# Two experts' weight loads per layer placed behind the overflow branch and the first gathered tokens

## The chip, the cores and the metric

The kernel runs on one NeuronCore of a Trainium2 chip. The metric is the device time of one execution in microseconds, as the median of several runs. Matrix products run on TensorE (PE in the profile; PEld is its weight load), elementwise work on VectorE (DVE), ScalarE (ACT) and GpSimd (POOL). SyncE (SP) issues nearly all DMA transfers; POOL issues the indirect ones.

## The reference, cut to what matters

The reference is a transformer block followed by a second model of two layers. Each of these layers ends with a mixture of experts, and only that part is touched:

```python
MOE_GROUPS, MOE_EXPERTS_PER_GROUP, MOE_TOPK, D_EXPERT, D_MODEL = 4, 4, 2, 256, 1024
# a router picks a group of four experts for each token, and the best two in it
# for each token t and each of its two experts e, with weight c:
#     y[t] += c * ((silu(h[t] @ gate[e]) * (h[t] @ up[e])) @ down[e])
```

There are 16 experts; layer 0 has 768 tokens, layer 1 has 512. Everything is float32.

## The kernel before, in words

The program is one Python class that emits instructions for all engines into a tile framework. The framework inserts the semaphores from the tiles that an instruction reads and writes, and it orders the instructions of an engine by when it expects them to be ready, within what their tiles allow. So a DMA issue may stand earlier in SP's queue than where the Python code calls it, if nothing that it needs forbids it.

Each layer's expert stage has three parts.

The first, `moe_open`, `moe_chunk` and `moe_in`, runs beside and after the attention's output projection. `moe_in` finishes the router's logits; `route` turns them into a list of tokens for each slot: a prefix sum by a matmul with a triangular constant (L2410; in layer 0 the constant `tr` is loaded at L2373 and cast at L2375), a chain of small VectorE instructions, and the list `tok` (L2473). Meanwhile the normalized tokens are transposed, evicted into one of three row buffers `hgs` (L2354) and written to DRAM as `hrows` (L2355). The scaled tokens that are transposed lie in the buffers of the expert `ME[i]`, which is 2 in layer 0 and 3 in layer 1 (`mxa`).

The second, `moe`, works in blocks of 128 slots, one block for each of the 16 experts. `gather(b)` (L2589) fetches a block's rows of `hrows` by an indirect DMA on POOL into `hgs[b % 3]`. A block transposes them (L2609), splits them and the weights into a rounded part and a remainder (L106, L2580, L2581), multiplies with three matmuls for each product (L110 to L112), and scatters the result to `ybuf` (L2640). `blocks` interleaves the steps of neighbouring blocks: a block's weights are loaded up to three blocks ahead, its rows are gathered two ahead.

Before the 16 regular blocks there is a branch (L2655) on the number of overflow blocks, for experts with more than 128 tokens. With these inputs it is not taken: 32 gathers run, 16 in each layer. The gathers of blocks 0 and 1 are issued ahead of it. Its body would load experts into the buffers of expert `ov`, reload that expert afterwards and gather blocks 0 and 1 again. So what reads or writes the row buffers or `ov`'s weights after the branch can't be placed ahead of it; other work can.

The third sums up the two rows of each token from `ybuf`.

Weights: `load_expert(i, b)` issues ten loads on SP, eight for gate and up (four tiles `wgu`, two loads each, L2557) and two for down (`wd`, L2559). There are four sets of buffers (`ew`, expert `b` in set `b % 4`). The first four experts of a layer are loaded in different places:

- Layer 0: expert 0 in `moe_open`, expert 1 within the output projection, expert 3 in `moe_in`, and expert 2 (whose buffers hold the scaled tokens) in `moe` after the branch.
- Layer 1: expert 0 in the attention, expert 1 in `moe_open`, expert 2 within the output projection (after its first quarter), and expert 3 (whose buffers hold the scaled tokens) in `moe` after the branch.

Experts 4 to 15 follow as buffers come free. In the queue of SP, the eight gate and up loads of the expert that the code loads after the branch stand ahead of it, since they don't depend on it.

Of the kernel before, what the change touches and what calls it, by code (L numbers as in the profile page):

```python
# [37 lines left out]
ME = (2, 3)  # L38
# [6 lines left out]
NE, LD, NL = 4, 3, 4  # L45
# [5 lines left out]
class Model:  # L51
# [2000 lines left out]
    def layer1(self, mod):  # L2052
        nc, tc, I, c2 = self.nc, self.tc, self.I, self.c2
        X = self.X
        W = I["od_w_in_2"][0]
        self.l1w.close()
        snk = self.bcast_load(I["swa_sink_2"][0], 16, "snk1", c2)
        nsnk = self.t(c2, [128, 16], "nsnk1")
        nc.vector.tensor_scalar(nsnk, snk, -1.0, None, op0=ALU.mult)
        self.dflt = "st"  # L2060
        ep = self.l1p[1]
        bp = self.l1x.enter_context(tc.tile_pool(name="l1b", bufs=1, side="right"))
        band = self.t(bp, [128, 1664], "bandm")
        self.bandm = [band[:, 0:512], band[:, 512:1152], band[:, 1152:1664]]
        for case, m in enumerate(self.bandm):
            nc.sync.dma_start(m, I["c_band"][:, case, :m.shape[1]])
        oF = self.out_tiles(1, 2, 4)

        def q_unit(j):
            cst = self.t(ep, [128, 256], "cq", bufs=1)  # L2070

            def mm():
                raw = self.l1_load(W[:, 256 * j:256 * j + 256])
                self.l1_const(j, cst)
                while self.apr < 2 * j - 2:
                    yield
                self.newQ2(j)
                yield
                ps = self.bank("a2")
                out = [ps[:, t * 256:(t + 1) * 256] for t in range(4)]  # L2080
                for k0 in range(0, 8, 2):
                    hi, lo = (self.t(self.wp, [128, 512], t, F32R, bufs=3).rearrange("p (k n) -> p k n", n=256)
                              for t in ("whi", "wlo"))
                    self.l1_split(raw, 0, hi, lo, k0)
                    for k in range(k0, k0 + 2):
                        Hk, Lk = (T[k // 2][:, k % 2] for T in self.l1T)
                        for t in range(4):
                            sl = slice(t * 128, (t + 1) * 128)
                            for i, (a, b) in enumerate(((Hk, hi), (Hk, lo), (Lk, hi))):
                                nc.tensor.matmul(out[t], a[:, sl], b[:, k - k0], start=k == 0 and t % 2 == 0 and i == 0,  # L2090
                                                 stop=k == 7 and t % 2 == 1 and i == 2, skip_group_check=True)
                    yield
                return out

            def tile_(ps, t):
                raw = self.t(ep, [128, 256], "rawq", bufs=4)
                nc.vector.scalar_tensor_tensor(raw, ps[t], self.l1rs[:, t:t + 1], cst, op0=ALU.mult, op1=ALU.add)
                yield from self.l1_heads(raw, 4)
                yield
                yield from self.l1_queries(raw, t, self.Q2[j])  # L2100
            return ("q", j), mm, self.staged(4, tile_, 4)
        done = {("q", 0)}
        self.apr = 0
        filler = self.stream([lambda j=j: q_unit(j) for j in range(1, 4)], done, SL)
        with self.psum(st=3, s2=1, a2=1, pv=1), tc.tile_pool(name="l1a", bufs=1) as at:
            self.mark("attn1")
            self.band_attn(at, oF, snk, nsnk, filler, done)
        self.l1x.close()
        with self.psum(acc=5, lg=1, st=2):
            with tc.tile_pool(name="l1x", bufs=1) as xp:  # L2110
                self.pad(xp, 64)
                oT = (self.t(xp, [128, 8, 512], "oThi", F32R), self.t(xp, [128, 8, 512], "oTlo", F32R))
                wo = I["od_w_out_2"][0]
                first = self.primed(self.proj_feat_g(oT, [wo[:, 0:256]], 1024))
                for m in range(8):
                    self.split(oT[0][:, m, :], oT[1][:, m, :], oF(m, 0, 512))
                self.mq = xp
                self.moe_open(1, X, 4, [self.AB["f", 1, 0]])
                for nq in range(4):
                    pf = self.run_g(first) if nq == 0 else self.proj_feat(oT, [wo[:, nq * 256:(nq + 1) * 256]], 1024)  # L2120
                    for f in range(2):
                        d = nq * 2 + f
                        nc.vector.scalar_tensor_tensor(X[:, d, :512], pf[f], mod[:, 16 + d, 0:1], X[:, d, :512],
                                                       op0=ALU.mult, op1=ALU.add)
                        self.moe_chunk(d)
                    if nq == 0:
                        self.load_expert(1, 2)
            self.mark("moein1")
            self.moe_pool(1)
            self.moe_in(1)  # L2130
        self.mark("moe1")
        self.moe(1, mod, X, 4, None, None, None)
        self.xes.close()
# [159 lines left out]
    def moe_in(self, i):  # L2293

        nc, nt, lg = self.nc, self.mnt, self.lg
# [25 lines left out]
                nc.vector.tensor_reduce(L[:, n0:n0 + m], src.rearrange("p n g e -> p n e g"), axis=AX.X, op=ALU.add)  # L2321
        nc.vector.tensor_tensor(L, L, r[:, :, None].to_broadcast([128, nt, 20]), op=ALU.mult)
        nc.vector.tensor_tensor(L, L, self.lc, op=ALU.add)
        for j in range(NL):
            if j not in self.ewt and j != ME[i]:
                self.load_expert(i, j)
        self.hrows = self.dr.tile([nt * 128, 1024], F32, name=f"hrows{i}")

        rt, rth = self.t(mp, [128, nt], "rt"), self.t(mp, [128, nt, 3], "rth", F32R)
# [214 lines left out]
            return v[:, u, :] if nm is None else v[:, u:u + nm, :]  # L2544
        return at

    def load_expert(self, i, b, ev=None, into=None):

        nc, I, ep = self.nc, self.I, self.ew[b % NE]
        s1, s2 = (slice(b * n, (b + 1) * n) if ev is None else bass.ds(ev * n, n) for n in (1024, 256))  # L2550
        src = lambda nme: I[f"exp_w_{nme}_2"][i].rearrange("g e d f -> (g e d) f")
        gu, dn = into or ([self.t(ep, [128, 2, 512], f"wgu{c}") for c in range(4)],
                          [self.t(ep, [128, 1024], f"wd{k}") for k in range(2)])
        for c, w in enumerate(gu):
            for u, nme in enumerate(("gate", "up")):
                rows = src(nme)[s1, :].rearrange("(k p) n -> p k n", p=128)
                nc.sync.dma_start(w[:, :, u * 256:(u + 1) * 256], rows[:, 2 * c:2 * c + 2, :])  # L2557
        for k, w in enumerate(dn):
            nc.sync.dma_start(w, src("down")[s2, :].rearrange("(k p) n -> p k n", p=128)[:, k, :])  # L2559
        self.ewt[b] = gu, dn  # L2560

    def moe(self, i, mod, xT, nt, banks, begin, finish):
        nc, tc, I = self.nc, self.tc, self.I
# [2 lines left out]
        ybuf = self.dr.tile([2 * 768, 1024], F32, name=f"ybuf{i}")  # L2566
        hgs = self.hgs
        direct = 15 if i else None
        ov = 5 - ME[i]
        with self.ewx, tc.tile_pool(name=f"moel{i}", bufs=1) as mp, self.psum(st=3, ht=1, gu=2, yy=2):  # L2570
            self.pad(mp, 64)
            cnt = [0]
# [15 lines left out]
            def gather(b):  # L2588
                nc.gpsimd.indirect_dma_start(out=hgs[b % 3], out_offset=None, in_=self.hrows[:, :],  # L2589
                                             in_offset=bass.IndirectOffsetOnAxis(ap=self.tok[:, b:b + 1], axis=0),  # L2590
                                             bounds_check=T - 1, oob_is_err=False)
# [52 lines left out]
            def blocks(bs):  # L2644
                g = [block(b) for b in bs]
                for it in range(-3, len(g) + 2):
                    for d in (1, 0, -2, -1, 0, 2, LD):
                        if 0 <= it + d < len(g):
                            next(g[it + d], None)
# [5 lines left out]
            with tc.If(nov > 0):  # L2655
# [3 lines left out]
                self.load_expert(i, ov, into=self.ewt[ov])  # L2659
                for b in range(2):  # L2660
                    gather(b)
            self.load_expert(i, ME[i])
            blocks(range(16))
            if i:
                self.moe_end(mod, xT, ybuf, dS)
# [105 lines left out]
def host_consts():  # L2771
# [18 lines left out]
    for li, L in enumerate((64, 32, 16, 8, 4, 2, 1)):  # L2790
# [28 lines left out]
        "c_rope": np.ascontiguousarray(rope.transpose(1, 0, 2, 3)).astype(np.float32),  # L2819
        "c_band": band,  # L2820
        "c_moe": moe,
        "c_iota": np.ascontiguousarray(np.broadcast_to(a.astype(np.float32), (128, 128))),
        "c_onehot": oh,
# [28 lines left out]
```

## Time and profile before

| | |
|---|---|
| median of 3 runs | 2259.61 us (2256.55 to 2264.92) |
| profiled execution, its own time | 2261.34 us |
| its span, first to last instruction | 2259.6 us |
| TensorE busy | 94% of the span |
| granted clock, mean | 0.974 of full speed |
| expert stage of layer 0, first to last transpose of tokens | 1585.1 to about 1719 us |
| expert stage of layer 1, the same | 2077.4 to about 2211 us |

All times within the profile are counted from the span's start. A wait is named after the event that came last by the profile. `DMA share` is the mean busy share of the core's 16 DMA engines; the profile's estimate can lie a little above 1.

### The profile page before, as it was taken

What the parts mean: (1) busy time and instruction counts of PE and PEld (TensorE: products, weight loads), DVE (VectorE), ACT (ScalarE), POOL (GpSimd) and SP (SyncE); (2) the same over time, 40 slices, a digit from 0 to 9 for tenths busy, and PEclk for the clock granted to TensorE, in tenths of its full rate; (3) what the DMA queues carried; (4) which work ended last, traced back from release to release, by engine and by line L of the source; (5) the groups of instructions that cost most, each with busy time, mean ns of one, the idle gap of its engine ahead of it and who ended that gap; (6) DMA issues with size and microseconds to landing.
All of it is one profiled execution on the core that took longest, in us unless ns stands there. A gap on an engine that the chain in (4) does not pass through costs nothing. (4 is left out here: it accounts for less than half of the span.)

```text
span 2259.6 us, 36705 instructions
## 1 busy us (share of the span) xinstructions
PE 2125.8 (94%) x13410; PEld 1751.8 (78%) x13410; DVE 1401.2 (62%) x3175; ACT 1221.0 (54%) x2623; POOL 500.5 (22%) x459
## 2 busy tenths in 40 slices
PE   7999999999999999999999989896999989996997
PEld 6887775688887888888889777775787978775886
DVE  5665656555555544355631677644999777755997
ACT  4655456543334243333442676733898467654996
POOL 2222030002112212120420333100442421101442
PEclk9999999999999999999999999998999999998998
DMA  6446627553242222323112111064996411144995
GB/s 210 158 138 200 221 97 253 187 187 128 94 149 94 76 94 94 112 83 123 52 59 81 40 43 48 26 206 163 339 359 234 174 40 60 40 150 142 341 334 191
DMA packets 213120, 328.54 MB, mean 145 GB/s; under 512 B 22598, under 2 KB 150516, under 8 KB 206780
## 3 DMA queue, kind: packets, MB, share of 16 engines
q1 hardware_dynamic: 203708, 305.05, 40.3%
q0 software_dynamic: 9216, 20.99, 2.5%
q8 instruction: 109, 1.79, 0.3%
q14 instruction: 87, 0.71, 0.1%
HBM read 307.51 MB, written 31.06 MB: 150 GB/s over the span
## 5 line engine op out<-in xcount | busy, mean ns | idle before, releaser
L106 DVE TENSOR_TENSOR wlo<-wst,whi 128x512 fp32r<-128x512 f32 (+1 forms) x342 | 245.1, 722 | 418.6 <-ACT whi L105 355.8
L105 ACT CAST whi<-wst 128x512 fp32r<-128x512 f32 (+1 forms) x342 | 210.7, 619 | 486.0 <-PE acc L111 357.1
L112 PE MATMUL acc<-hThi,wlo 128*128 128x512 f32 (+2 forms) x576 | 225.3, 391 | 1.0 <-DVE wlo L106 0.9
L110 PE MATMUL acc<-hThi,whi 128*128 128x512 f32 (+2 forms) x576 | 225.0, 391 | 0.7 <-ACT ostg L633 0.7
L111 PE MATMUL acc<-hTlo,whi 128*128 128x512 f32 (+2 forms) x576 | 224.5, 390 | 0.0
L153 POOL TENSOR_TENSOR hnr<-rsq,nhalf 128x4 f32<-128x4 f32 (+3 forms) x58 | 72.2, 1245 | 266.5 <-DVE rsq L147 144.4
L218 PE MATMUL acc<-whi,hThi 128*128 128x256 f32 x416 | 122.3, 294 | 6.5 <-ACT hThi L374 6.2
L112 PEld LDWEIGHTS acc<-hThi,wlo 128*128 128x128 f32 (+2 forms) x576 | 106.8, 185 | 25.9 <-DVE wlo L106 2.5
L524 PE MATMUL pv<-PT,V 128*64 128x128 f32 x1456 | 123.1, 283 | 3.1 <-ACT PT L1469 1.7
L110 PEld LDWEIGHTS acc<-hThi,whi 128*128 128x128 f32 (+2 forms) x576 | 106.8, 185 | 24.5 <-issue 2.9
L111 PEld LDWEIGHTS acc<-hTlo,whi 128*128 128x128 f32 (+2 forms) x576 | 106.8, 185 | 20.9
L218 PE MATMUL acc<-wlo,hThi 128*128 128x256 f32 x416 | 119.9, 288 | 0.0
L218 PE MATMUL acc<-whi,hTlo 128*128 128x256 f32 x416 | 119.4, 288 | 0.0
L524 PEld LDWEIGHTS pv<-PT,V 128*64 128x64 f32 x1456 | 88.8, 138 | 28.5 <-issue 12.1
L112 PE MATMUL acc<-hMhi,wlo 128*128 128x512 f32 x256 | 99.9, 391 | 1.3 <-DVE wlo L106 1.3
L110 PE MATMUL acc<-hMhi,whi 128*128 128x512 f32 x256 | 100.2, 391 | 0.0
L111 PE MATMUL acc<-hMlo,whi 128*128 128x512 f32 x256 | 99.6, 389 | 0.0
L2581 DVE TENSOR_TENSOR elo<-wgu,ehi 128x512 fp32r<-128x512 f32 x128 | 89.2, 706 | 11.6 <-ACT ehi L2580 10.9
L218 PEld LDWEIGHTS acc<-whi,hThi 128*128 128x128 f32 x416 | 81.1, 195 | 12.1 <-ACT hThi L374 6.5
L2580 ACT CAST ehi<-wgu 128x512 fp32r<-128x512 f32 x128 | 80.8, 631 | 1.7
L2580 ACT CAST whi<-wgu 128x512 fp32r<-128x512 f32 x128 | 81.1, 634 | 0.6 <-PE gu L112 0.2
L218 PEld LDWEIGHTS acc<-wlo,hThi 128*128 128x128 f32 x416 | 81.2, 195 | 0.3 <-DVE wlo L106 0.2
(701 smaller groups left out, 6146.1 us busy)
## 6 DMA issues: line engine op xcount, KB each, us to landing
mst<-in_mod_w_dram SPq DMA_DIRECT2D x48, 1024.0 KB
wgu<-in_exp_w_gate_dram SPq DMA_DIRECT2D x128, 256.0 KB
wgu<-in_exp_w_up_dram SPq DMA_DIRECT2D x128, 256.0 KB
wd<-in_exp_w_down_dram SPq DMA_DIRECT2D x64, 512.0 KB
wst<-in_w_in_dram SPq DMA_DIRECT2D x22, 1024.0 KB
wst<-in_w_up_dram SPq DMA_DIRECT2D x16, 1024.0 KB
wst<-in_w_down_dram SPq DMA_DIRECT2D x16, 1024.0 KB
wst<-in_od_w_in_dram SPq DMA_DIRECT2D x10, 1024.0 KB
```

The source lines that it names most:

```text
L105: nc.scalar.copy(hi, src)
L106: nc.vector.tensor_tensor(lo, src, hi.bitcast(F32), op=ALU.subtract)
L110: mm(ps, A[0], B[0], start=start, stop=False)
L111: mm(ps, A[0], B[1], start=False, stop=False)
L112: mm(ps, A[1], B[0], start=False, stop=stop)
L153: nc.gpsimd.tensor_tensor(out, m, self.nhalf[:p, :n], op=ALU.pow)
L218: self.nc.tensor.matmul(out[t], A[x], B[y], start=kc == 0 and t % 2 == 0 and i == 0, stop=last and i == 2, skip_group_check=True)
L524: self.nc.tensor.matmul(out[64 * a:64 * a + 64], *pairs[a][k], start=k == 0, stop=k == n - 1, tile_position=(0, 64 * a), skip_group_check= ...
L2580: nc.scalar.copy(hi, w)
L2581: (nc.gpsimd if pool else nc.vector).tensor_tensor(lo, w, hi.bitcast(F32), op=ALU.subtract)
```

## The change

- Experts 2 and 3 of both layers are now loaded in `moe` after the branch, 2 first. The calls in `moe_in` (layer 0's expert 3) and in layer 1's output projection (expert 2) are gone; experts 0 and 1 are loaded where they were.
- `load_expert` gets an argument `behind`. With it, POOL copies two elements per partition from that tile into each `wgu` tile (one for each of the tile's two loads in that row) and one into each `wd` tile before the loads are issued: six copies for each expert, twelve in a layer. The tile is `hgs[0]`, the rows that block 0 gathered. So each of these loads waits for a copy, and each copy for the gather and for the branch.
- `ov`, the expert whose buffers the overflow body uses and reloads, becomes 1 in both layers (it was 3 and 2).

```diff
--- before.py
+++ after.py
@@ -2123,8 +2123,6 @@
                         nc.vector.scalar_tensor_tensor(X[:, d, :512], pf[f], mod[:, 16 + d, 0:1], X[:, d, :512],
                                                        op0=ALU.mult, op1=ALU.add)
                         self.moe_chunk(d)
-                    if nq == 0:
-                        self.load_expert(1, 2)
             self.mark("moein1")
             self.moe_pool(1)
             self.moe_in(1)
@@ -2321,9 +2319,6 @@
                 nc.vector.tensor_reduce(L[:, n0:n0 + m], src.rearrange("p n g e -> p n e g"), axis=AX.X, op=ALU.add)
         nc.vector.tensor_tensor(L, L, r[:, :, None].to_broadcast([128, nt, 20]), op=ALU.mult)
         nc.vector.tensor_tensor(L, L, self.lc, op=ALU.add)
-        for j in range(NL):
-            if j not in self.ewt and j != ME[i]:
-                self.load_expert(i, j)
         self.hrows = self.dr.tile([nt * 128, 1024], F32, name=f"hrows{i}")
 
         rt, rth = self.t(mp, [128, nt], "rt"), self.t(mp, [128, nt, 3], "rth", F32R)
@@ -2544,13 +2539,18 @@
             return v[:, u, :] if nm is None else v[:, u:u + nm, :]
         return at
 
-    def load_expert(self, i, b, ev=None, into=None):
+    def load_expert(self, i, b, ev=None, into=None, behind=None):
 
         nc, I, ep = self.nc, self.I, self.ew[b % NE]
         s1, s2 = (slice(b * n, (b + 1) * n) if ev is None else bass.ds(ev * n, n) for n in (1024, 256))
         src = lambda nme: I[f"exp_w_{nme}_2"][i].rearrange("g e d f -> (g e d) f")
         gu, dn = into or ([self.t(ep, [128, 2, 512], f"wgu{c}") for c in range(4)],
                           [self.t(ep, [128, 1024], f"wd{k}") for k in range(2)])
+        if behind is not None:
+            for w in gu:
+                nc.gpsimd.tensor_copy(w[:, 0, ::256], behind[:, 0:2])
+            for w in dn:
+                nc.gpsimd.tensor_copy(w[:, 0:1], behind[:, 0:1])
         for c, w in enumerate(gu):
             for u, nme in enumerate(("gate", "up")):
                 rows = src(nme)[s1, :].rearrange("(k p) n -> p k n", p=128)
@@ -2566,7 +2566,7 @@
         ybuf = self.dr.tile([2 * 768, 1024], F32, name=f"ybuf{i}")
         hgs = self.hgs
         direct = 15 if i else None
-        ov = 5 - ME[i]
+        ov = 1
         with self.ewx, tc.tile_pool(name=f"moel{i}", bufs=1) as mp, self.psum(st=3, ht=1, gu=2, yy=2):
             self.pad(mp, 64)
             cnt = [0]
@@ -2659,7 +2659,8 @@
                 self.load_expert(i, ov, into=self.ewt[ov])
                 for b in range(2):
                     gather(b)
-            self.load_expert(i, ME[i])
+            for j in range(2, NL):
+                self.load_expert(i, j, behind=hgs[0])
             blocks(range(16))
             if i:
                 self.moe_end(mod, xT, ybuf, dS)
```

## Rows read from the trace of the kernel before

**Rows 1.** Chain that ended last, around the two routers: start us, us, what.

```profile
1555.53 8.14 DMA tr<-in_c_tris_dram
...
1572.35 12.62 another core or an unknown queue
...
2067.19 10.09 another core or an unknown queue
```

**Rows 2.** Windows: us, busy us (instructions) of PE, PEld, DVE, ACT, POOL, PEclk, DMA share, GB/s.

```profile
1552.00:1557.00 5.00, 4.49 (x35) 3.63 (x34) 3.25 (x19) 1.94 (x5) 1.32 (x1) 1.00 0.96 310
...
1567.00:1590.00 23.00, 5.98 (x32) 5.22 (x33) 10.25 (x30) 8.72 (x15) 5.86 (x7) 0.50 0.74 257
...
1586.00:1590.00 4.00, 4.00 (x17) 3.62 (x16) 2.83 (x4) 3.48 (x7) 3.43 (x4) 0.50 0.94 330
1590.00:1720.00 130.00, 130.00 (x636) 107.14 (x635) 127.05 (x219) 121.90 (x235) 55.55 (x39) 1.00 1.03 363
...
1722.00:1725.00 3.00, 3.00 (x15) 2.48 (x14) 3.00 (x6) 2.49 (x4) 0.00 (x0) 1.00 0.33 132
...
2090.00:2210.00 120.00, 119.91 (x582) 98.48 (x581) 118.32 (x204) 112.04 (x218) 51.11 (x36) 1.00 0.98 338
...
2077.00:2085.00 8.00, 7.58 (x32) 6.76 (x33) 6.57 (x11) 6.19 (x12) 4.54 (x4) 0.68 0.63 203
...
2000.00:2020.00 20.00, 20.00 (x87) 15.38 (x86) 9.21 (x15) 9.29 (x17) 0.00 (x0) 1.00 1.05 348
```

**Rows 3.** Timeline of DVE in layer 0's router: start us, us, what, idle before.

```profile
1564.36 0.26 DVE L2414 COPY tot<-st 128x96 f32<-128x96 f32 x1 [4.29 <-PE st L2411]
```

**Rows 4.** Timeline of PE in the same place.

```profile
1562.26 0.48 PE L2352 MATMUL acc<-mB,mrow 128*128 128x512 f32 x1
```

**Rows 5.** Timeline of SP: expert 15's last slice, and layer 1's loads before the branch.

```profile
1713.91 0.37 SPq L2557 DMA_DIRECT2D wgu<-in_exp_w_up_dram  x1
...
2063.57 0.39 SPq L2557 DMA_DIRECT2D wgu<-in_exp_w_gate_dram  x1
...
2205.09 0.37 SPq L2557 DMA_DIRECT2D wgu<-in_exp_w_up_dram  x1
```

**Rows 6.** Timeline of POOL: the second gather of layer 1.

```profile
2068.87 1.01 POOL L2589 DMA_INDIRECT hg<-hrows,tok  x1 [0.17 <-POOLq L2655]
```

**Rows 7.** Line L2655, the branch: ns min/median/max, first to last start us.

```profile
L2655 POOLq EVENT_SEMAPHORE  x5: 17/43/8057, 1576.4 to 1576.7; - x5
...
L2655 POOLq EVENT_SEMAPHORE  x5: 17/43/7254, 2068.9 to 2069.2; - x5
```

**Rows 8.** By tile: scatters near 1730 and 2222, a gather near 1596.

```profile
DMA to landing us min/median/max: 3.3/3.3/3.3
...
DMA to landing us min/median/max: 4.4/4.4/4.4
...
DMA to landing us min/median/max: 7.0/7.0/7.0
```

**Rows 9.** Timeline of ACT: expert 15's last slice; first work after layer 1's branch.

```profile
1729.57 0.63 ACT L2580 CAST ehi<-wgu 128x512 fp32r<-128x512 f32 x1
...
2074.22 1.28 ACT L2580 ACT_TABLE_LOAD   x1 [9.84 <-DVEq L2655]
...
2221.63 0.63 ACT L2580 CAST ehi<-wgu 128x512 fp32r<-128x512 f32 x1
```

**Rows 10.** Small POOL operations, by tile: ns min/median/max.

```profile
L97 POOL MEMSET pad<- x8: 101/120/180, 1.4 to 2068.6; 128x16 f32 x5, 128x56 f32 x1, 128x48 f32 x1, 128x40 f32 x1
...
L2041 POOL COPY V<-raw x6: 289/292/488, 1767.5 to 1815.2; 128x128 f32<-128x128 f32 x6
```

**Rows 11.** Timeline of PE: first transposes, and those of block 2.

```profile
1585.10 2.79 PE L2609 MATMUL st<-ident,hg 128*128 128x128 f32 x12 [12.76 <-remote]
...
1595.01 1.03 PE L2609 MATMUL st<-ident,hg 128*128 128x128 f32 x8
```

**Rows 12.** Timeline of PE: expert 15's last slice is multiplied.

```profile
1732.61 0.39 PE L110 MATMUL gu<-ehi,gThi 128*128 128x512 f32 x1
```


## The prediction

> **What bounds the kernel now.** The table above has TensorE busy 94% of the span, so I looked for the places where it is not, and began with the chain of waits around the two expert stages [rows 1]. In layer 0's router the small constant `tr`, issued at 1555.53 behind expert 3's ten loads, holds the chain for 8.14 us. After the router each layer stands still (12.62 and 10.09 us) until the first gathered tokens are in; the chain calls the releaser unknown, and POOL's own waits below show that it is the two gathers. Then I read the windows of both stages [rows 2]. Past the first gather TensorE has no gap (130.00 of 130 us, 119.91 of 120), although DMA is full all the while (share 1.03 and 0.98). So the start of each expert stage is bound by latency, its body by TensorE, and DMA has almost nothing left over there.
>
> **Part 1, layer 0's router (expert 3 leaves `moe_in`).** Its ten loads go. They waited for the same memory as `tr`, so `tr` can be issued some 5 us earlier, with no 3.15 MB ahead of it. What is late next: VectorE stood 4.29 us before its chain to the token list, which starts at 1564.36 [rows 3], so with a handoff at most 4.2 us is won. At least 1.5 us is won, if TensorE keeps its order, in which the prefix matmul follows a pair of transposes whose last part starts at 1562.26 [rows 4]. The row buffers' writes, which shared the DMA with these loads and which the gather needs too, also get quicker. I take 3.8 us, near the upper end, since the instruction order is made from expected readiness and `tr` is no longer late.
>
> **Part 2, the first gathers land earlier (both layers).** Eight loads (2.10 MB) of the expert that follows the branch are issued just before the gathers, in layer 1 from 2063.57 on [rows 5], with the second gather at 2068.87 [rows 6]; layer 0 has the same eight. After the change nothing is ahead of the gathers. POOL waits at the branch L2655 for both of them: 8.06 us from 1576.7, and 7.25 us from 2069.2 [rows 7]. The second gather started 0.3 us earlier than that in layer 1, so it took some 8.4 and 7.6 us. What an indirect transfer takes with DMA empty is not shown for a gather; a lone scatter of the same shape landed after 3.3 us in layer 0 and 4.4 us in layer 1, a gather among weight loads after 7.0 us [rows 8]. Two gathers lie behind each other, so I take 4.2 and 4.4 us: won are 4.2 and 3.2 us. The bounds: 1.4 and 0.6 us (the contended 7.0), 5.1 and 3.2 us (a lone scatter). Layer 1 has a second bound: ScalarE's first work stood 9.84 us until VectorE had come past the branch, at 2074.22 [rows 9]; if that jump is no quicker with DMA empty, the table load and three casts that ScalarE does before it needs the tokens leave about 1.4 us of the gain. Sum of parts 1 and 2: 3.8 + 4.2 + 3.2 = 11.2 us, bounds 1.5 + 1.4 + 0.6 = 3.5 and 4.2 + 5.1 + 3.2 = 12.5.
>
> **Part 3, the copies.** Twelve per layer on POOL, of two elements per partition or one. No row has that shape; a 128x16 fill takes 0.12 us and a 128x128 copy 0.29 us [rows 10], so 12 take 1.4 to 3.5 us; I take 2.4. Queued behind them on POOL are the gathers of blocks 2, 3 and 4 and the split of one weight slice. TensorE reads block 2's tokens at 1595.01, 9.9 us after its first transpose (1585.10) [rows 11]. With 1.0 for the gather instruction [rows 6], 2.4 for the copies and 7.0 to land it comes 0.5 us late (between 0 and 1.6). I cost this at nothing, since part 4 makes TensorE wait later for the same DMA anyway; without that cover it is 0.5 us per layer.
>
> **Part 4, the loads come into a full stage.** Layer 0 had expert 3 whole and eight loads of expert 2 under way ahead of its first transpose; layer 1 had expert 2 whole, loaded in the output projection, and eight loads of expert 3 [rows 5]. All of it now follows the landing of the gather: in each layer 3.15 + 2.10 = 5.24 MB more in the stage itself. Leaving the output projection wins nothing there: TensorE is busy 20.00 of 20 us while DMA is full (1.05) [rows 2]. Blocks 2 and 3 still come in time: eight loads need about 2.1/0.31 = 7 us, and block 2's weights are wanted some 16 us in, after two blocks of about 9 us less the lead of the splits. But from there DMA never gets ahead again. The price of 5.24 MB: at the stage's own rate (363 and 338 GB/s) 14.4 and 15.5 us, at that of the weight loads alone (310 GB/s, 1552 to 1557) 16.9 us [rows 2]. I take 14.9 and 15.6, nearer the stage's own rate, since the mix is its own. DMA also starts later after the first transpose. In layer 0 it ran at 0.94 from one microsecond after it [rows 2]; now a copy, an issue and a transfer's latency of nearly 2 us (a lone scatter's 3.3 less 1.4 for at most 0.52 MB) come first, some 2.3 us, so 1.4 us more. In layer 1 DMA was only 0.63 busy over 2077 to 2085 [rows 2], 3.0 us idle, so 0.2 us more; I give these two 1.0 to 1.8 and -1.5 to 0.5. The last loads thus land 16.3 and 15.8 us later, counted from the first transpose.
>
> What spare time takes this up? In layer 0 the last gate/up slice of expert 15 is issued at 1713.91, with two 512 KB loads behind it [rows 5]. DMA runs dry between 1722 and 1725 (0.33) [rows 2], so that slice lands 2.9 us before (1.05 MB at 363), at 1719.1 to 1722.1; I take 1720.8. It is cast at 1729.57 (0.63 us) and multiplied at 1732.61 [rows 9, 12]. Cast, an equally long low part and handoffs need some 1.6 us, so 1.4 of the 3.04 us between is spare too: 1731.0 - 1720.8 = 10.2 us (8.9 to 11.9). In layer 1 the slice is issued at 2205.09 and cast at 2221.63 [rows 5, 9]; by the same 6.9 us from issue to landing, 2223.0 - 2212.0 = 11.0 us (9.5 to 12). TensorE is held up by 16.3 - 10.2 = 6.1 us in layer 0 and 15.8 - 11.0 = 4.8 us in layer 1, in pieces of 1 to 3 us over about the last four blocks. Bounds: layer 0 14.4 + 1.0 - 11.9 = 3.5 to 16.9 + 1.8 - 8.9 = 9.8; layer 1 15.5 - 1.5 - 12 = 2.0 to 16.9 + 0.5 - 9.5 = 7.9. Sum 10.9 us, 5.5 to 17.7.
>
> **A rule against this price.** The 130 us window shows 363 GB/s at a share of 1.03, so DMA gives no more in this mix [rows 2]. The Trainium skill, "DMA: Bandwidth & Descriptors", section "Bandwidth", has 425 GB/s measured for a 16 MB transfer while the neighbour core idles. By that rate the 5.24 MB would cost an estimated 12.3 us per layer, and the stage would never have fallen behind; the rows contradict it here.
>
> **The sum.** -11.2 + 10.9 = -0.3 us on the profiled execution's 2261.34 us (its span is 2259.6). That execution lies 1.7 us above the median of the runs, so I forecast 2259.61 - 0.3, some 2259 us.
>
> **Rivals.** *The body hides everything (faster).* If the loads keep ahead, only -11.2 is left: 2248 us. For it: TensorE had no stall in spite of the full DMA. Against: the spare of 10 to 11 us at the last block is less than the 16 us added. It decides by the rate: up to layer 0's last slice some 49.6 MB of before (363 over 1590 to 1722, 330 over the 4 us ahead, 132 over the 3 us behind [rows 2]) + 5.24 - 1.05 = 53.8 MB must pass in 1731.0 - 1585.1 - 2.3 = 143.6 us, or 375 GB/s against the 363 seen; that is near. The skill's 425 GB/s would lead here too.
>
> *The gathers gain nothing.* If their time is their own and not the loads', part 2 falls to 2.0 us and the sum is -5.8 + 10.9: 2264.7 us. For it: a gather amid loads takes just 7.0 us. Against: the lone scatters.
>
> *The late waits also cost the clock (slower).* TensorE's granted clock is 0.50 (1.2 GHz) over 1567 to 1590, after it stood nearly idle [rows 2], and the first 5 us of work still run at that level. If the waits of part 4 are long enough to drop it, each fall costs about 2.5 us (5 us at half speed); two or three per layer, less what the waits hide, give +12 to +16: 2271 to 2276 us. It decides if a single wait for a slice is several microseconds rather than 1 to 3. The Trainium skill, "TensorE: Matmul & The Clock Gate", Part 1, says that the throttled level is the default and activity releases it; the 0.50 bears that out, so this rival is a mechanism to reckon with.
>
> *The change does not do what it says.* If the copies and loads are placed elsewhere in the queues, so that the loads still meet the gathers, the time stays within 3 us of 2259.6.
>
> **How the numbers follow.** 0.5% of 2259.6 is 11.3 us, about what can be told from no change. Forecast as summed (2251 to 2268): 0.53, of which 0.03 faster. Body hides everything: 0.20, about 0.12 of it beyond 2248.3. Gathers gain nothing: 0.12, of which 0.02 slower. Clock: 0.10, all slower. Not what it says: 0.05, inside. So faster 0.15, same 0.73, slower 0.12. The bounds of the terms give 5.5 - 12.5 = -7.0 and 17.7 - 3.5 = +14.2; with the rivals, and no more than 2 in 10 left out, the range is 2248 to 2271.
>
> **What would show it.** Right: `tr` issued near 1551; VectorE's chain starting near 1560.5; POOL's wait at the branch about 4 us instead of 8.06 and 7.25; DMA full from the copies to the end of each stage, and running dry some 8 us nearer to TensorE's last block; new idle of TensorE on late weights in blocks 12 to 15 of each layer, 5 to 6 us. Wrong: no new idle there (then faster), the granted clock below 1.00 in the body (then slower), or POOL's wait unchanged.

## The result, and the profile after

The changed kernel takes 2272.5 us, median of 6 (2269.2 to 2280.39), against 2259.07 us, median of 6, for the kernel before: ratio 1.0054, interval 1.0038 to 1.007, so 12.2 us slower (8.6 to 15.8). That is 1.5 us above the forecast's range. The profiled execution of the changed kernel is the slowest of its six. Its span (2278.6 us) is 19.0 us longer than that of the kernel before, and 9.0 us of these arise ahead of layer 0's router, where both kernels issue the same instructions. So all comparisons below are of stretches counted from a mark inside the stage.

| stretch (profiled executions) | before | after | measured | forecast |
|---|---|---|---|---|
| layer 0: start of the router (copy into `lT`) to first gather | 24.19 | 20.39 | -3.80 | -3.8 |
| layer 0: first gather to first transpose of tokens | 10.54 | 7.88 | -2.66 | -4.2 |
| layer 0: first to last transpose of tokens | 133.6 | 142.8 | +9.2 | +6.1 |
| layer 1: start of the router to first gather | 16.73 | 16.73 | 0 | 0 |
| layer 1: first gather to first transpose | 9.98 | 7.51 | -2.47 | -3.2 |
| layer 1: first to last transpose | 133.6 | 143.4 | +9.8 | +4.8 |
| sum of both stages | 328.6 | 338.7 | +10.1 | -0.3 |

The marks of layer 0's front are these: ScalarE's copy into `lT` and POOL's first gather in the kernel before, and the same copy in the changed kernel (its first gather stands further below, at 1579.78).

```profile
1550.37 0.58 ACT L2303 COPY lT<-lg 64x512 f32<-64x512 f32 x1 [0.68 <-DVE ssq L2286]
...
1574.56 1.26 POOL L2589 DMA_INDIRECT hg<-hrows,tok  x1 [0.99 <-issue]
...
1559.39 0.58 ACT L2301 COPY lT<-lg 64x512 f32<-64x512 f32 x1 [0.68 <-DVE ssq L2284]
```

Both fronts are shorter and both bodies longer, as forecast; the bodies lost 19.0 us where 10.9 were expected. First the chain of waits (start us, us, what), which answers to [rows 1]:

```profile
1568.57 0.23 DVE As L2400
1568.85 0.20 PE st L2405
...
1577.06 10.47 another core or an unknown queue
...
1633.74 9.07 DMA wgu<-in_exp_w_up_dram
1642.83 9.18 DMA wgu<-in_exp_w_up_dram
1652.02 12.86 DMA wgu<-in_exp_w_up_dram
...
2079.66 7.62 another core or an unknown queue
```

The constant `tr` has left the chain: the prefix matmul follows its input `As` with no gap. The standstills ahead of the first transposes are shorter (10.47 and 7.62 against 12.62 and 10.09). But now the chain runs through weight loads all along both bodies, where in the kernel before it ran through TensorE's work; three loads of layer 0 are shown. Each of them is issued when the one before it on the chain has landed (1642.83 + 9.18 = 1652.01). The windows (columns as in [rows 2]) show what that does to TensorE:

```profile
1590.00:1650.00 60.00, 60.00 (x293) 49.52 (x292) 58.92 (x99) 55.97 (x107) 27.17 (x21) 0.98 1.03 360
1650.00:1740.00 90.00, 82.80 (x384) 66.72 (x383) 79.53 (x137) 75.15 (x145) 30.43 (x23) 0.98 1.03 363
1664.00:1666.00 2.00, 0.05 (x1) 0.00 (x0) 0.09 (x1) 1.03 (x3) 0.00 (x0) 1.00 0.82 273
1668.00:1670.00 2.00, 2.00 (x9) 1.81 (x8) 1.81 (x5) 2.00 (x6) 1.76 (x2) 0.50 1.04 377
1740.00:1743.00 3.00, 3.00 (x16) 2.43 (x15) 2.92 (x5) 2.95 (x7) 2.63 (x2) 1.00 0.27 108
...
2140.00:2230.00 90.00, 84.53 (x394) 67.93 (x393) 80.40 (x139) 76.01 (x146) 31.19 (x24) 0.98 0.98 340
```

For the first 60 us TensorE has no gap; over the next 90 it stands 7.20 us, in layer 1 5.47 us. Its longest stop is 2.94 us (up to 1666.99, in a row below), and one microsecond after it TensorE works at a granted clock of 0.50. DMA moves the same 363 and 340 GB/s as before, at the same full share.

VectorE's chain and POOL's branch, which answer to [rows 3, 6 and 7]; the gathers' landing times answer to [rows 8], the first line layer 0, the second layer 1. VectorE's chain now starts without a wait, 9.74 us after the router's start instead of 13.99.

```profile
1569.13 0.26 DVE L2409 COPY tot<-st 128x96 f32<-128x96 f32 x1
...
L2655 POOLq EVENT_SEMAPHORE  x5: 17/43/5384, 1581.6 to 1582.0; - x5
...
L2655 POOLq EVENT_SEMAPHORE  x5: 17/43/4870, 2081.2 to 2081.6; - x5
```

```profile
DMA to landing us min/median/max: 5.0/5.5/6.0
...
DMA to landing us min/median/max: 4.5/4.8/5.1
```

```profile
1579.78 1.27 POOL L2589 DMA_INDIRECT hg<-hrows,tok  x1 [1.50 <-issue]
1581.35 0.99 POOL L2589 DMA_INDIRECT hg<-hrows,tok  x1 [0.31 <-SPq L2655]
1587.76 0.55 POOL L2551 COPY wgu<-hg 128x2 f32<-128x2 f32 x4 [5.41 <-remote]
1588.24 0.31 POOL L2553 COPY wd<-hg 128x1 f32<-128x1 f32 x2
1588.48 0.57 POOL L2551 COPY wgu<-hg 128x2 f32<-128x2 f32 x4
1588.96 0.33 POOL L2553 COPY wd<-hg 128x1 f32<-128x1 f32 x2
1589.42 1.01 POOL L2589 DMA_INDIRECT hg<-hrows,tok  x1
```

With hardly anything beside them the two gathers, issued 1.6 us apart, land 5.0 and 6.0 us after issue in layer 0, 4.5 and 5.1 in layer 1, and POOL stands 5.38 and 4.87 us at the branch instead of 8.06 and 7.25. The twelve copies take 1.5 us (1587.76 to 1589.29). The first transposes follow, with those of block 2 9.67 us behind them (9.91 in [rows 11]), with no wait; the third line is TensorE's longest stop:

```profile
1587.66 2.79 PE L2609 MATMUL st<-ident,hg 128*128 128x128 f32 x12 [10.60 <-remote]
...
1597.33 1.03 PE L2609 MATMUL st<-ident,hg 128*128 128x128 f32 x8
...
1666.99 0.50 PE L111 MATMUL yy<-wlo,dThi 128*128 128x512 f32 x1 [2.94 <-DVE wlo L2581]
```

The first and the last transpose, by line (ns min/median/max, first to last start us), give the length of the bodies, first in the kernel before, then in the changed one, each time layer 0 and layer 1:

```profile
L2609 PE MATMUL st<-ident,hg x128: 272/273/445, 1585.1 to 1718.7; 128*128 128x128 f32 x128
...
L2609 PE MATMUL st<-ident,hg x128: 272/273/446, 2077.4 to 2211.0; 128*128 128x128 f32 x128
...
L2609 PE MATMUL st<-ident,hg x128: 270/273/444, 1587.7 to 1730.5; 128*128 128x128 f32 x128
...
L2609 PE MATMUL st<-ident,hg x128: 271/273/448, 2087.4 to 2230.8; 128*128 128x128 f32 x128
```

Last the weight slices: SP's issue of the last gate/up slice of experts 7 and 15 of layer 0 and of expert 15 of layer 1, then ScalarE's first casts of them (with the first slice of expert 8 between). They answer to [rows 5 and 9].

```profile
1649.31 0.37 SPq L2557 DMA_DIRECT2D wgu<-in_exp_w_up_dram  x1
...
1733.74 0.37 SPq L2557 DMA_DIRECT2D wgu<-in_exp_w_up_dram  x1
...
2232.22 0.37 SPq L2557 DMA_DIRECT2D wgu<-in_exp_w_up_dram  x1
```

```profile
1658.58 0.62 ACT L2580 CAST ehi<-wgu 128x512 fp32r<-128x512 f32 x1 [1.06 <-DMA wgu<-in_exp_w_up_dram]
1664.97 0.62 ACT L2580 CAST ehi<-wgu 128x512 fp32r<-128x512 f32 x1 [3.16 <-DMA wgu<-in_exp_w_up_dram]
...
1741.64 0.63 ACT L2580 CAST ehi<-wgu 128x512 fp32r<-128x512 f32 x1
...
2241.35 0.63 ACT L2580 CAST ehi<-wgu 128x512 fp32r<-128x512 f32 x1
```

Expert 7's last slice is cast 9.27 us after its issue, and ScalarE stood 1.06 us for it. In the kernel before the same slice was issued and cast here, 30.39 us apart:

```profile
1623.80 0.38 SPq L2557 DMA_DIRECT2D wgu<-in_exp_w_up_dram  x1
```

```profile
1654.19 0.65 ACT L2580 CAST ehi<-wgu 128x512 fp32r<-128x512 f32 x1
```

I took this distance, the lead of a load over its use, for the last slice of several experts, from the same two views:

| last gate/up slice of expert | 4 | 7 | 10 | 12 | 13 | 15 |
|---|---|---|---|---|---|---|
| layer 0 before, issue to cast, us | 32.6 | 30.4 | 23.5 | 18.6 | 17.6 | 15.7 |
| layer 0 after | 13.7 | 9.3 | 9.2 | 9.1 | 7.9 | 7.9 |
| layer 1 before | 32.2 | 30.9 | 25.2 | 19.6 | 18.5 | 16.5 |
| layer 1 after | 14.8 | 10.2 | 9.0 | 9.5 | 9.6 | 9.1 |

This table is the core of the case. In the kernel before, from expert 7 to 15, the last slices are issued every 11.26 us ((1713.91 - 1623.80)/8) and cast every 9.42 us ((1729.57 - 1654.19)/8): DMA is slower than TensorE, and the stage lives on a head start that shrinks with every block and just lasts. That the loads wait mostly for DMA and not for free buffers is to be seen in SP's queue: from 1620 to 1715 it stood 49.4 us in the kernel before, 37.4 of them until an earlier load had landed and 12.0 until VectorE was done with something. Two of the lines (us in total, times, longest us):

```profile
SPq L2557 <- DMA wgu<-in_exp_w_gate_dram: 10.2, 19, 1.8
...
SPq L2557 <- DVE wlo L2581: 4.7, 5, 2.1
```

The change takes 17 to 19 us off that head start at expert 4. In layer 0 nothing is left of it from expert 7 on, in layer 1 from expert 8, and in layer 0 casts come every 10.38 us, at the pace of the loads (10.55). That loads come every 10.55 us now and came every 11.26 before may be because slower blocks bring fewer gathers and scatters between them; this is argued, not shown.

### The profile page after: what moved, and what is told of

Read it like the earlier page. It is cut to its first block, busy times and chain, and to the rows that moved or that the text cites. A ratio compares the mean times of both kernels' runs of the same rounds, so it can differ in the third digit from the quotient of the medians.

```text
span 2278.6 us, 36608 instructions
## 1 busy us (share of the span) xinstructions
PE 2137.1 (94%) x13410; PEld 1756.5 (77%) x13410; DVE 1404.2 (62%) x3175; ACT 1222.0 (54%) x2623; POOL 499.2 (22%) x483
## 5 line engine op out<-in xcount | busy, mean ns | idle before, releaser
L2581 POOL TENSOR_TENSOR wlo<-wgu,whi 128x512 fp32r<-128x512 f32 x32 | 50.7, 1584 | 144.7 <-ACT whi L2580 128.7
```

Source lines behind the costliest of these rows:

```text
L2581: (nc.gpsimd if pool else nc.vector).tensor_tensor(lo, w, hi.bitcast(F32), op=ALU.subtract)
```

## The experiments

An expert is called tied when its loads wait for POOL's copies from the gathered rows, as experts 2 and 3 do in the changed kernel.

The stretches of all runs, as in the table above (layer 0: router to first gather, first gather to first transpose, first to last transpose; layer 1: the last two; then the sum of both stages against the kernel before and the timed difference, from the ratio's interval). The expectations counted to the start of the last group of transposes instead of the last one, so their bodies are 0.4 to 0.6 us shorter:

| run | to gather | to transpose | body 0 | to transpose | body 1 | stages, us | time, us |
|---|---|---|---|---|---|---|---|
| before | 24.19 | 10.54 | 133.6 | 9.98 | 133.6 | 0 | 0 |
| changed | 20.39 | 7.88 | 142.8 | 7.51 | 143.4 | +10.1 | +8.6 to +15.8 |
| e1 | 25.33 | 9.22 | 133.5 | 10.09 | 133.2 | -0.6 | -3.4 to +4.7 |
| e2 | 23.72 | 7.71 | 136.0 | 7.75 | 134.6 | -2.1 | -6.8 to +1.6 |
| e3 | 20.44 | 7.73 | 133.6 | 7.16 | 133.9 | -9.1 | -9.7 to -2.7 |
| e4 | 20.44 | 9.35 | 133.2 | 10.34 | 133.6 | -5.0 | -6.8 to +0.7 |
| e5 | 20.65 | 7.79 | 151.1 | 7.51 | 149.8 | +24.9 | +16.7 to +29.9 |
| e6 | 20.36 | 9.36 | 133.5 | 7.58 | 134.3 | -6.8 | -2.0 to +4.8 |
| e7 | 20.46 | 11.39 | 133.1 | 7.52 | 135.1 | -4.4 | -9.1 to -3.2 |
| e8 | 20.43 | 7.59 | 136.9 | 7.58 | 135.4 | -4.1 | -2.3 to +5.9 |
| e9 | 20.21 | 9.67 | 133.2 | 7.35 | 134.4 | -7.1 | -7.7 to -2.3 |
| e10 | 20.10 | 10.65 | 133.7 | 7.53 | 134.4 | -5.6 | -7.0 to -1.4 |
| e11 | 20.18 | 10.51 | 133.6 | 7.38 | 134.5 | -5.8 | -3.8 to +1.6 |

**e1, the router alone** (on the kernel before):

```diff
-        for j in range(NL):
-            if j not in self.ewt and j != ME[i]:
-                self.load_expert(i, j)
...
         late = self.route(i, mp, L, nt)
+        for j in range(NL):
+            if j not in self.ewt and j != ME[i]:
+                self.load_expert(i, j)
```

> The kernel before with one move: layer 0's ten loads of expert 3 are issued after the router's code instead of ahead of it, so the constant tr no longer stands behind them. The same bytes are loaded ahead of the branch as before. My theory (the router's part of the gain is tr alone): the second gather of layer 0 starts 3.5 to 4.5 us earlier relative to the start of the router, the expert stages are unchanged, and the time is 2255 us, 3.8 below the kernel before. Rival (the ten loads only collide later, with the writes of the token rows and with the gathers): within 1.5 us of the kernel before.

Ratio 1.0003 (0.9985 to 1.0021); the rival holds. VectorE's chain does start 4.2 us sooner after the router's start (9.74 against 13.99 us), but the ten loads still stand ahead of the six writes of the token rows, and the gather waits for those. POOL's timeline:

```profile
1574.73 0.11 POOL L97 MEMSET pad<- 128x16 f32 x1 [15.91 <-ACT hg L2354]
1580.77 1.26 POOL L2589 DMA_INDIRECT hg<-hrows,tok  x1 [5.92 <-DMA hrows<-hg]
```

So moving `tr` ahead is not enough by itself; in the changed kernel the gain of 3.8 us needs the loads out of the writes' way too.

**e2, one expert tied** (on the kernel before, with the new argument `behind` and its copies):

```diff
-            self.load_expert(i, ME[i])
+            self.load_expert(i, ME[i], behind=hgs[0])
```

> The kernel before with the copies for one expert alone, the one that it loads after the branch already (2 in layer 0, 3 in layer 1); all other loads stay where they were. 2.10 MB per layer come into the stage instead of 5.24. In both theories the second gather takes about 6.3 us instead of 8.4 and 7.6: 3.4 us are won in all. Theory A (the spare time of 10 to 11 us at the last block is usable, 2.10 MB at 363 and 338 GB/s are 5.8 and 6.2 us and so hidden): 2255.7 us. Theory B (the stage's loads are already just in time at each block, so added bytes cost their full time wherever they come): 2.10/5.24 of the 20 us that the whole change lost in the two stages, 8 us, less 3.4: 2263.7 us, with TensorE waiting on weights around blocks 7 to 13.

Ratio 0.9989 (0.997 to 1.0007). That excludes theory B's 4.6 us of loss, and theory A's 3.4 us of gain lies within the interval; the stages lie between the two: 5.5 us won at the fronts, 2.4 and 1.0 lost in the bodies. The waits come at experts 12 and 14 in layer 0, late, as a head start that runs out late would have it. ScalarE:

```profile
1694.71 0.63 ACT L2585 CAST ehi<-wgu 128x512 fp32r<-128x512 f32 x1 [0.43 <-DMA wgu<-in_exp_w_up_dram]
1697.62 0.62 ACT L2585 CAST ehi<-wgu 128x512 fp32r<-128x512 f32 x1 [1.50 <-DMA wgu<-in_exp_w_up_dram]
1700.09 0.62 ACT L2585 CAST ehi<-wgu 128x512 fp32r<-128x512 f32 x1 [0.84 <-DMA wgu<-in_exp_w_up_dram]
1719.73 0.62 ACT L2585 CAST ehi<-wgu 128x512 fp32r<-128x512 f32 x1 [0.54 <-DMA wgu<-in_exp_w_up_dram]
```

The spare time is usable, against theory B, but smaller than theory A had it.

**e3, two loads fewer** (on the changed kernel; the weights of experts 4 and 5 are left out):

```diff
+                elif b in (4, 5):
+                    self.ewt[b] = self.ewt[b - 4]
                 elif b >= NL:
```

> The changed kernel, which here leaves out the loads of experts 4 and 5 in both layers (blocks 4 and 5 multiply with the weights of experts 0 and 1, so their result is not the reference's). Copies, tie and order stay; each stage has 6.29 MB less to load than the changed kernel, 1.05 MB less than the kernel before. Theory (the loss of about 20 us in the two stages is the bytes in a full DMA queue): no idle of TensorE on weights, granted clock 1.00 in both bodies, and what is left is the gain at the fronts, 8.8 us below the kernel before: 2250 us, 2248 to 2253. Rival (the copies on POOL, the late start of the loads or the changed order of SP's queue cost it): waits at blocks 7 to 13 remain, 2262 us or more.

Ratio 0.9973 (0.9957 to 0.9988), so 6.1 us below the kernel before; the two stages are 9.1 us shorter. The copies, the tie and the late start are all still there, and the bodies are as long as before. Windows of both bodies:

```profile
1583.00:1712.00 129.00, 128.90 (x627) 106.02 (x626) 127.22 (x216) 120.99 (x232) 55.28 (x39) 1.00 1.03 363
2073.00:2201.00 128.00, 127.48 (x621) 104.64 (x620) 126.24 (x216) 119.70 (x230) 56.36 (x39) 1.00 0.99 339
```

TensorE stands 0.1 and 0.5 us, and its clock is full. This shows that the loss in the bodies comes from the bytes, and that the copies, the tie and the late start cost nothing where DMA keeps ahead.

**e4, the changed kernel without the copies:**

```diff
-                self.load_expert(i, j, behind=hgs[0])
+                self.load_expert(i, j)
```

> The changed kernel without the copies: experts 2 and 3 are loaded after the branch in the code, but nothing ties the loads to the gather, so 17 of layer 0's 20 loads and all but two of layer 1's stand ahead of the branch in SP's queue. Theory (the tie is what moves the bytes into the stage): bodies of the two stages as in the kernel before, no idle on weights; tr is early, worth 3.8 us; the gathers take the 8.4 and 7.6 us of before: 2255 us. Rival (where the code calls the loads matters more than the tie): bodies 5 us or more longer in each layer, 2265 us or more.

Ratio 0.9987 (0.997 to 1.0003). The bodies are those of before and the gathers keep about their old length, 9.35 and 10.34 us to the first transpose against 10.54 and 9.98; the router's gain stays whole. Here only six of expert 3's loads stand ahead of the row writes, against ten in e1. It is the copies that move the bytes, not the place in the code.

**e5, three experts tied** (on the changed kernel):

```diff
-                    if nq == 0:
-                        self.load_expert(0, 1)
...
-        self.load_expert(i, i)
+        if i == 0:
+            self.load_expert(i, i)
...
-        ov = 1
+        ov = 0
...
-            for j in range(2, NL):
+            for j in range(1, NL):
```

> The changed kernel with one expert more behind the gather: expert 1's loads, too, are tied to the gathered rows in both layers, 3.15 MB more in each stage. Theory (from block 7 on the stage runs at the pace of DMA, 10.7 to 11 us for an expert against 9.6 us of work, and no spare time is left): the added bytes cost their whole time at 363 and 338 GB/s, 8.7 and 9.3 us. First to last transpose of tokens then is 151 and 152 us instead of 142.3 and 142.8, and the time 2290 us (18 above the changed kernel). Rival (the waits come from the uneven order in which the slices arrive, and a later start hides in waits that are there already): less than 5 us in each layer, 2281 us at most.

2289.22 us, ratio 1.0103 (1.0074 to 1.0132); bodies of 151.1 and 149.8 us, 8.3 and 6.4 above the changed kernel, 8.7 and 9.3 expected. So with the lead spent, 3.15 MB more cost nearly their whole transfer time in layer 0 and two thirds of it in layer 1. It is the bodies that exclude the rival's "less than 5 us": the time, 16.7 to 29.9 us above the kernel before in four executions, would still allow its 22 us. The windows show no faster DMA, and TensorE's idle time on top:

```profile
1609.00:1735.00 126.00, 116.32 (x541) 93.40 (x539) 110.53 (x189) 103.64 (x201) 42.90 (x33) 0.97 1.04 365
2115.00:2235.00 120.00, 111.22 (x517) 89.65 (x517) 105.46 (x181) 99.31 (x192) 42.94 (x35) 0.97 1.00 345
```

**e6 and e11, one expert tied, the other untied and behind `tr`** (on the changed kernel, the same code twice):

```diff
-                self.load_expert(i, j, behind=hgs[0])
+                self.load_expert(i, j, behind=hgs[0] if j == ME[i] else None)
```

> The changed kernel with the copies for one expert alone (2 in layer 0, 3 in layer 1); the other's loads stand behind tr in layer 0 and in the output projection in layer 1, untied. Theory (the parts add up as measured one by one): router -3.8 us, first gather to first transpose -2.8 and -2.3, first to last transpose +2.4 and +1.0, so 5.5 us below the kernel before, 2255.5 us. Rival (the other expert's last four loads, 1.5 MB, stand just ahead of layer 0's branch and take that gather's gain): 2258 us, with 9.3 us or more from layer 0's first gather to the first transpose.

> The kernel with one expert tied and tr early, once more. Its two stages were 6.4 us shorter than before in the profiled execution, its time was not (1.0006). Theory (the time was an unlucky draw of what varies ahead of the first router, where the instructions are the same): 0.996 to 0.999 of the kernel before this time. Rival (the placement itself lengthens something outside the two stages): 1.000 or more again.

Ratios 1.0006 (0.9991 to 1.0021) and 0.9995 (0.9983 to 1.0007), while the profiled stages are 6.8 and 5.8 us shorter. The layer-0 gather lost its gain, as the rival had it (9.36 and 10.51 us to the first transpose). In time, e6 gained neither the theory's 5.5 us nor the rival's 3, and e11's median lies between its two forecasts. Why the time shows less than the stages stays open, here and in e8 below: in e11's profile the stretch between the stages is 2.5 us longer than before (335.00 against 332.55), but it is so in e10, too, whose time agrees with its stages.

**e7 and e10, half of that expert tied** (as e6, and the same code twice):

```diff
-            for w in gu:
+            for w in gu[2:]:
                 nc.gpsimd.tensor_copy(w[:, 0, ::256], behind[:, 0:2])
```

> As the run with one expert tied and tr early, but only two of that expert's four gate/up tiles and its down tiles are tied; the other four loads (1.05 MB) stand ahead of the branch. Theory (a stage has about 7.5 us of lead to spend, and up to there added bytes are free): first to last transpose 133.1 to 133.5 us in both layers, as before; the gathers keep half of their gain, -1.4 and -1.1 us; with the router's -3.8 the time is 2255 us, 6 below the kernel before. Rival (every byte costs in proportion): first to last transpose about 134.3 and 133.6 us, 2256.5 us or more.

> The kernel with half of one expert tied, once more beside the other two. Theory: its two stages are 4.4 us shorter than before, and so is the time, 0.997 to 0.999 of the kernel before. Rival (its 0.9973 was a lucky draw of what varies ahead of the first router): 0.999 or more, with the start of layer 0's router past 1553 us in the profiled execution.

Ratios 0.9973 (0.996 to 0.9986) and 0.9982 (0.9969 to 0.9994): 4 to 6 us below the kernel before, and so below the changed one. But not for the reason given: layer 0's gather gains nothing (11.39 and 10.65 us), and layer 1's gains all of what a whole tie brings. Layer 0's body is as before; layer 1's is 1.5 and 0.8 us longer.

**e8, one load fewer, in the middle** (on the changed kernel; the weights of expert 10 are left out):

```diff
+                elif b == 10:
+                    self.ewt[b] = self.ewt[b - 4]
                 elif b >= NL:
```

> The changed kernel, which here leaves out the load of expert 10 in both layers (block 10 multiplies with expert 6's weights, so its result is not the reference's): 3.15 MB less, in the middle of the stage. Theory (from block 7 on each block is late by what DMA needs more than TensorE, some 1.2 us, until the lead comes back): blocks 7 to 10 lose 3.5 to 4.5 us, then an expert's load of 10.9 us is won back and lasts for the five blocks that are left, so first to last transpose is about 137 us in each layer, 5.5 less than in the changed kernel, and the time 2262 us. Rival (the loss is one late start, made good or not by the queue's order): waits return at blocks 12 to 14 and the stretch stays at 140 us or more, 2268 us.

2263.22 us, ratio 1.0008 (0.999 to 1.0026). Bodies of 136.9 and 135.4 us, where 137 and, by the rival, 140 were expected. ScalarE's waits for slices in layer 0 are these three, at experts 8 and 9, and none after the load that was left out:

```profile
1656.88 0.62 ACT L2580 CAST ehi<-wgu 128x512 fp32r<-128x512 f32 x1 [1.49 <-DMA wgu<-in_exp_w_up_dram]
1659.27 0.62 ACT L2580 CAST ehi<-wgu 128x512 fp32r<-128x512 f32 x1 [0.76 <-DMA wgu<-in_exp_w_up_dram]
...
1668.57 0.62 ACT L2580 CAST ehi<-wgu 128x512 fp32r<-128x512 f32 x1 [0.50 <-DMA wgu<-in_exp_w_up_dram]
```

So the loss is not one late start: it grows block by block while the lead is spent, and stops when the lead is given back. The time (-2.3 to +5.9 us against the kernel before) excludes the rival's 2268 us, 8.9 above it, and allows the theory's 2262.

**e9, one expert tied in layer 1 alone** (on the changed kernel):

```diff
-                self.load_expert(i, j, behind=hgs[0])
+                self.load_expert(i, j, behind=hgs[0] if i and j == ME[i] else None)
```

> The changed kernel with the copies in layer 1 alone, and there for expert 3 alone; layer 0's loads are untied and stand behind tr. Theory (the stretches measured one by one add up): layer 0 as in the untied run, 5.3 us shorter from the start of its router to the last transpose than in the kernel before; layer 1 as in the runs with one expert tied, 1.2 to 1.4 us shorter; sum -6.6, 2255 us against 2261.5. Rival (layer 1's tie costs in time what it gains at the front, as the run with one expert tied in both layers hints): -4 us, 2258 us.

2256.65 us, ratio 0.9978 (0.9966 to 0.999), so -5.0 us (-7.7 to -2.3), which does not tell theory from rival; the stages, 7.1 us shorter, agree with the theory. With the version of e7 and e10 it is one of two that beat both kernels, by about 0.2%; e9 was run once: early `tr`, row writes less hindered, and at most one expert tied where the lead can pay for it.

## Why the prediction was wrong, step by step

**What bounds the kernel.** That the body is bound "by TensorE, and DMA has almost nothing left over there" was only half of it. DMA was the slower of the two already, 11.26 against 9.42 us per expert, and TensorE was not late only because of the head start. That was to be read in the kernel before, from an early slice beside the last one; I looked at the last one alone.

**Part 1 held:** `tr` was issued when the router began, VectorE's chain no longer waited, -3.80 us against -3.8. That it fits so well is in part luck: the chain starts 4.25 us sooner, and 0.45 of it is lost again before the gather. e1 adds what I had only named in passing: without the row writes getting quicker, nothing is won.

**Part 2, the gathers, was too hopeful:** -2.66 and -2.47 us for -4.2 and -3.2. I took a lone scatter's landing (3.3 and 4.4 us) as the measure; the two gathers, 1.6 us apart and beside hardly anything else, took 4.5 to 6.0. The Trainium skill, "DMA: Bandwidth & Descriptors", section "Anatomy of one DMA — SWDGE (gpsimd) path", has about 2.0 us plus the bytes at 436 GB/s, an estimated 3.2 us for these 0.52 MB; the measured times are longer, and they decide.

**Part 3 held:** 1.5 us of copies for 2.4, and nothing waits for them: block 2's tokens are read 9.67 us after the first transpose, 9.91 before.

**Part 4 is the step that failed, in the size of its terms.** Its mechanism stands: moved bytes cost their transfer time less the spare time. Counted from the first transpose, the last slice is issued 17.3 us later than before (146.08 - 128.81), and 17.1 us in layer 1, where I had 16.3 and 15.8. The spare time was 10.2 and 11.0 us in my sum; the lead of that slice shrank by only 7.8 and 7.4 us (15.66 to 7.90, 16.54 to 9.13). So it is cast 9.5 and 9.7 us later instead of 6.1 and 4.8, and the bodies lost 9.2 and 9.8.

The spare time was also read at the wrong place. I took it at the last slice, where DMA is about to run dry and a load landed within some 6.9 us. But no cast waited for that slice. The waits came in blocks 7 to 12 of layer 0 and 8 to 13 of layer 1, not in the last four, every block or two once the lead was gone; there the queue was full, and the three loads of the chain shown above took 9.1 to 12.9 us from issue to landing. The account is settled at expert 12 in layer 0: its last slice is issued 18.8 us later, its lead falls from 18.6 to 9.1, and it is cast 9.3 us later, nearly the whole loss. That the lead is what counts is shown by e8 and e3, in which the waits end or fail to come when it is given back, and by e2, in which they begin when it has run out.

**The rivals.** "The body hides everything" needed 375 GB/s; over the long windows of layer 0's body all runs shown stayed at 360 to 365. The Trainium skill, "DMA: Bandwidth & Descriptors", section "Bandwidth", gives, besides the 425 GB/s, about 358 for each of two cores that stream from the same memory at once. The rows lie near that (360 to 365 in layer 0, 338 to 345 in layer 1), though one core runs here; no run shows what the limit is. "The late waits also cost the clock" gave the right time, 2271 to 2276, by luck, for mostly another reason: the granted clock did fall to 0.50 after the stop of 2.94 us, but over the 90 us of layer 0 it averages 0.98, an estimated loss of 1.8 us, beside 7.20 us in which TensorE had nothing to work on. In layer 1's 90 us it averages 0.98, too. As DMA sets the pace there, a slower TensorE may even have cost nothing; that is argued, not shown. "The gathers gain nothing" is excluded: POOL's wait fell by 2.7 and 2.4 us. "The change does not do what it says" is excluded by the result, in which no load of experts 2 and 3 stands ahead of the gathers (SP issues the first at 1587.97 and 2087.69); e4 shows that the copies are what holds the loads back.

**The range.** The bounds of the terms reached 14.2 us above the kernel before, or 2273.8 us, and the measured 2272.5 lies inside; the range was cut to 2271 by the chances given to slower outcomes. Of the terms, part 4 passed its own upper bound, 19.0 us against 17.7, and it did so in layer 1 (9.8 against 7.9; 9.2 against 9.8 in layer 0).

## What to carry to other kernels

A full DMA beside a gapless TensorE does not tell which of the two is the bound. Take the time from a load's issue to its use at an early, a middle and a late place of the loop: if it shrinks, and the issues wait for earlier transfers and not for free buffers, DMA is slower, the loop lives on a head start, and whatever spends the head start (a later start, more bytes) costs most of its time from the block at which it runs out. What a wait for a transfer wins at the front must be set against that, and moving less can win where moving all loses (e7, e9 and e10).

## What the runs showed of the hardware

- Two indirect gathers of 128 rows of 4 KB, 1.6 us apart and with hardly anything beside them, land 4.5 to 6.0 us after their issue; lone scatters of the same shape landed in 3.3 and 4.4 [rows 8].
- The expert stage's DMA gave 360 to 365 GB/s in layer 0 and 338 to 345 in layer 1 over its long windows, whether 12 (e3), 14 (the changed kernel) or 15 (e5) experts were loaded in it, and whether TensorE waited or not.
- Ahead of layer 0's router, where the kernel before and the changed one issue the same instructions, the time of arrival was 1550.37 and 1559.39 us in two executions, and all thirteen profiled lie between 1549.29 and 1559.39. A change of a few microseconds is better read within a stage than from the whole time.
